# Five of eight output stores put into the load ring, and the last weights cut into other pieces

## The chip, the cores and the metric

The kernel runs on one core of a Trainium2 chip. The metric is device microseconds of one execution: the median of several runs. One execution is also profiled; its span is the time from the first to the last instruction on the core, and its own time is a little longer than the span.

## The reference

Eight experts, each a two-layer network over 256 rows of its own; all tensors are float32.

```python
n_experts, capacity, hidden, expert_hidden = 8, 256, 512, 2048

def reference(x, w1, w2, b1, b2):
    h = np.matmul(x, w1) + b1[:, np.newaxis, :]
    h = np.maximum(h, 0)
    return (np.matmul(h, w2) + b2[:, np.newaxis, :]).astype(np.float32)
```

x is 8 x 256 x 512, w1 is 8 x 512 x 2048 and w2 is 8 x 2048 x 512. The weights are 4 MB for each expert and product, 67 MB in all; the output is 0.5 MB for each expert.

## The kernel before

**Loads.** The weights, and x of experts 2 to 7, are cast from float32 to float16 on their way into SBUF. Such DMAs are issued by GpSimd (lines 65, 71, 82 and 90) and go through one queue, q0 in the profile, in the order of issue; here it is called the ring. A w1 or w2 takes 2 MB in SBUF as float16. x of experts 0 and 1 and b1 come through the SyncE and ScalarE queues and are cast by VectorE.

**Products.** `first_product(e)` makes 16 groups of 4 matmuls (128x128 weights, 256 columns); each group's sum goes through ScalarE (bias and relu, line 117) into `hT[e]`. In its middle `transposes(e + 1)` turns the x of the next expert. `second_product(e)` starts two sums, one for each half of the rows (tb 0 and 1), with b2 (line 151) and adds 16 rows of w2 blocks to each (line 163; "rows" of w2 are the 16 values of j, 512 columns each). `store` then copies tb 0 with VectorE (line 130) and tb 1 with ScalarE (line 131) into a tile of `out_pool`, which has two buffers, and SyncE issues one DMA of 512 KB (line 137).

**Order.** Stage s runs `first_product(s)` and, three stages late (LAG), `second_product(s - 3)`. A list `loads` holds x, w1 and w2 in the order in which they are wanted, and at each stage `issue_until` writes out loads up to w1 of expert s + 2 and w2 of expert s - 1. Each w1, and each w2 but the last, has three buffers, so that GpSimd's issue waits until TensorE has done with the buffer's old content. GpSimd works through its issues in order; what stands behind a waiting one waits too. SyncE's stores wait in the same way for the two copies.

**The last expert.** Its w2 comes in six pieces in tiles of their own: rows 0-4, 4-8, 8-12 and 12-14 over all 512 columns, then rows 14-16 as two halves of 256 columns. There are two blocks of 256 columns with two sums each. When the piece with row 15 of a block has been added, that block is copied and stored, tb 0 by SyncE (line 134) and tb 1 by ScalarE's own queue (line 135). So ScalarE copies, issues, copies and issues.

Of the kernel before, what the change touches and what calls it, by code (L numbers as in the profile page):

```python
# [11 lines left out]
def kernel(  # L12
# [9 lines left out]
    nc = tc.nc  # L22
    fp32 = mybir.dt.float32
    fp16 = mybir.dt.float16
    E, T, H = x.shape
    M = w1.shape[2]
    P = 128
    nTB = T // P
    nKC = H // P
    nJ = M // P  # L30
    HH = H // 2
    LAG = 3
    nXF32 = 2

    def ordered(ins):
        return tc.keep_in_program_order(ins)

    singles = ctx.enter_context(tc.tile_pool(name="singles", bufs=1))
    w1_pool = ctx.enter_context(tc.tile_pool(name="w1", bufs=3))
    w2_pool = ctx.enter_context(tc.tile_pool(name="w2", bufs=3))  # L40
    w2t_pool = ctx.enter_context(tc.tile_pool(name="w2t", bufs=1))
    x_pool = ctx.enter_context(tc.tile_pool(name="xp", bufs=4))
    xT_pool = ctx.enter_context(tc.tile_pool(name="xTp", bufs=2))
    hT_pool = ctx.enter_context(tc.tile_pool(name="hT", bufs=LAG + 2))
    out_pool = ctx.enter_context(tc.tile_pool(name="outp", bufs=2))
    psum_x = ctx.enter_context(tc.tile_pool(name="psum_x", bufs=1, space=bass.MemoryType.PSUM))
    psum_h = ctx.enter_context(tc.tile_pool(name="psum_h", bufs=3, space=bass.MemoryType.PSUM))
    psum_o = ctx.enter_context(tc.tile_pool(name="psum_o", bufs=2, space=bass.MemoryType.PSUM))
# [10 lines left out]
    w1_sb = [None] * E  # L59
    w2_sb = [None] * E  # L60
    hT = [None] * E

    def load_x(e):
        x16[e] = x_pool.tile([P, nTB, H], fp16, tag="x16", name="x16")
        ordered(nc.gpsimd.dma_start(  # L65
            out=x16[e], in_=x[e].rearrange("(p tb) h -> p tb h", tb=nTB)
        ))
# [7 lines left out]
    def load_w2(e):  # L75
        src = w2[e].rearrange("(p j) h -> p j h", j=nJ)
        w2_sb[e] = []
        if e < E - 1:
            t = w2_pool.tile([P, nJ, H], fp16, tag="w2", name="w2sb")
            step = nJ if e < E - 2 else nJ // 2  # L80
            for lo in range(0, nJ, step):
                ordered(nc.gpsimd.dma_start(out=t[:, lo : lo + step, :], in_=src[:, lo : lo + step, :]))  # L82
                w2_sb[e].append((lo, lo + step, 0, H, t[:, lo : lo + step, :]))
            return
        for lo, hi, c0, c1 in (
            (0, 4, 0, H), (4, 8, 0, H), (8, 12, 0, H), (12, 14, 0, H),
            (14, 16, 0, HH), (14, 16, HH, H),
        ):
            t = w2t_pool.tile([P, hi - lo, c1 - c0], fp16, tag=f"w2_{lo}_{c0}", name=f"w2_{lo}_{c0}")
            ordered(nc.gpsimd.dma_start(out=t, in_=src[:, lo:hi, c0:c1]))  # L90
            w2_sb[e].append((lo, hi, c0, c1, t))

    def transposes(e):
        pt = psum_x.tile([P, nKC, T], fp16, tag="psx", name="psx")
        for kc in range(nKC):
            for tb in range(nTB):
                ordered(nc.tensor.transpose(  # L97
                    out=pt[:, kc, tb * P : (tb + 1) * P],
                    in_=x16[e][:, tb, :].rearrange("p (q kc) -> p q kc", kc=nKC)[:, :, kc],
                    identity=ident16,  # L100
                ))
        xT[e] = xT_pool.tile([P, nKC, T], fp16, tag="xT", name="xT")
        nc.vector.tensor_copy(out=xT[e], in_=pt)  # L103

    def first_product(e):
        hT[e] = hT_pool.tile([P, nJ, T], fp16, tag="hT", name="hT")
        for j in range(nJ):
            ph = psum_h.tile([P, T], fp32, tag="ph", name="ph")
            for kc in range(nKC):
                ordered(nc.tensor.matmul(  # L110
                    out=ph,
                    lhsT=w1_sb[e][:, kc, :].rearrange("p (q j) -> p q j", j=nJ)[:, :, j],
                    rhs=xT[e][:, kc, :],
                    start=(kc == 0),
                    stop=(kc == nKC - 1),
                ))
            nc.scalar.activation(  # L117
                out=hT[e][:, j, :],
                in_=ph,
                func=mybir.ActivationFunctionType.Relu,  # L120
                bias=b1T[:, j, e : e + 1],
                scale=1.0,
            )
            if j == nJ // 2 and e + 1 < E:
                transposes(e + 1)

    def store(e, po, c0, c1, split):
        w = c1 - c0
        out_sb = out_pool.tile([P, nTB, w], fp32, tag=f"out{w}", name=f"out{w}")
        nc.vector.tensor_copy(out=out_sb[:, 0, :], in_=po[0])  # L130
        nc.scalar.copy(out=out_sb[:, 1, :], in_=po[1])  # L131
        dst = out[e].rearrange("(p tb) h -> p tb h", tb=nTB)[:, :, c0:c1]
        if split:
            nc.sync.dma_start(out=dst[:, 0, :], in_=out_sb[:, 0, :])
            nc.scalar.dma_start(out=dst[:, 1, :], in_=out_sb[:, 1, :])  # L135
        else:
            nc.sync.dma_start(out=dst, in_=out_sb)

    def second_product(e):
        if e < E - 1:  # L140
            blocks = [(0, H, psum_o, "po")]
        else:
            blocks = [(0, HH, psum_o, "po"), (HH, H, psum_h, "ph")]
        acc = {}
        for c0, c1, pool, tag in blocks:
            for tb in range(nTB):
                t = pool.tile(
                    [P, c1 - c0], fp32, tag=tag if tag == "ph" else f"{tag}{tb}", name=f"acc{tb}"
                )
                acc[c0, tb] = t  # L150
                ordered(nc.tensor.matmul(  # L151
                    out=t,
                    lhsT=ones1,
                    rhs=b2_sb[0:1, e * H + c0 : e * H + c1],
                    start=True,
                    stop=False,
                ))
        for lo, hi, p0, p1, t in w2_sb[e]:
            mine = [b for b in blocks if p0 <= b[0] and b[1] <= p1]
            for tb in range(nTB):  # L160
                for j in range(lo, hi):
                    for c0, c1, _, _ in mine:
                        ordered(nc.tensor.matmul(  # L163
                            out=acc[c0, tb],
                            lhsT=hT[e][:, j, tb * P : (tb + 1) * P],
                            rhs=t[:, j - lo, c0 - p0 : c1 - p0],
                            start=False,
                            stop=(j == nJ - 1),
                        ))
            if hi == nJ:  # L170
                for c0, c1, _, _ in mine:
                    store(e, [acc[c0, tb] for tb in range(nTB)], c0, c1, e == E - 1)

    x32 = singles.tile([P, nXF32, nTB, H], fp32)
    for e in range(nXF32):
# [4 lines left out]
        out=b2_sb,  # L180
        in_=b2.rearrange("e h -> (e h)").rearrange("(o f) -> o f", o=1),
# [10 lines left out]
    for j in range(nJ):  # L192
        for s in range(2):
            ordered(nc.tensor.matmul(  # L194
                out=pb[s * 64 : (s + 1) * 64, j, :, :],
# [5 lines left out]
    for s in range(2):  # L201
        nc.vector.tensor_copy(  # L202
            out=b1T[s * 64 : (s + 1) * 64, :, :], in_=pb[s * 64 : (s + 1) * 64, :, :, s]
        )
    transposes(0)

    loads = []
    for s in range(1, E + LAG):
        if s < E:
            if s >= nXF32:  # L210
                loads.append((load_x, s))
            loads.append((load_w1, s))
        if s >= LAG:
            loads.append((load_w2, s - LAG))
    n = 0

    def issue_until(done):
        nonlocal n
        while n < len(loads) and not done():
            loads[n][0](loads[n][1])  # L220
            n += 1

    for s in range(E + LAG):
        issue_until(lambda: (
            (min(s + 2, E - 1) < E and w1_sb[min(s + 2, E - 1)] is not None)
            and (s + 2 < LAG or w2_sb[min(s + 2 - LAG, E - 1)] is not None)
        ))
        if s < E:
            first_product(s)
        if s >= LAG:  # L230
            second_product(s - LAG)


# [28 lines left out]
```

## Time and profile before

| | |
|---|---|
| median of 3 runs | 186.31 us (185.98 to 186.66) |
| profiled execution: its time / its span | 185.88 us / 183.9 us |
| busy: TensorE / ScalarE / VectorE / GpSimd | 75% / 34% / 7% / 9% |
| DMA: moved, mean rate | 40.57 MB, 221 GB/s |
| HBM read / written | 71.39 MB / 4.19 MB |
| mean granted TensorE clock | 0.922 |

The profile's page gives for each engine a busy time, and cuts the span into 40 slices with a digit for each (9 is 90% busy or more). For DMA it gives the mean busy share of the core's 16 DMA engines and the bytes per second; a casting load counts with what it writes, half of what it reads. A second table gives packets, megabytes and share of the DMA engines for each queue: q0 is the GpSimd ring, q1 SyncE's queue and q10 ScalarE's. The chain of work that ended last goes back from the last instruction, at each step to what released it. In a timeline a line gives the start, the length, the engine, the line of the kernel, what is written from what, how many instructions are merged, and in brackets the idle time before and what ended it. The trace also holds one record for each DMA packet (queue, size written, start, length) and the moment at which each DMA's landing was signalled; where a text speaks of packet records or landings, it means these.

Some groups of the page (line, engine, operation, count, busy time, mean of one in ns, idle time before it and its releaser):

```profile
L110 PE MATMUL ph<-xT,w1sb 128*128 128x256 f16 x512 | 69.3, 302 | 11.8 <-DMA w1sb<-in_w_dram 11.8
L117 ACT ACTIVATE hT<-ph,b1T 128x256 f16<-128x256 f32 x128 | 57.1, 475 | 47.4 <-PE ph L110 47.1
L163 PE MATMUL acc<-w2sb,hT 128*128 128x512 f16 x224 | 49.7, 379 | 1.5 <-DMA w2sb<-in_w_dram 1.5
L90 POOL DMA_DIRECT2D w<-in_w_dram x6 | 3.6, 614 | 12.4 <-DMA w2sb<-in_w_dram 12.4
```

### The profile page before, as it was taken

To read this page: it belongs to the slowest core of one execution; us is meant where nothing else is said; L and a number is where in the kernel's file an instruction comes from. 1 tells how busy PE (TensorE), PEld (TensorE's weight loads), DVE (VectorE), ACT (ScalarE), POOL (GpSimd) and SP (SyncE) were. 2 spreads that over 40 slices of the span, in tenths; PEclk is the share of its full clock that TensorE was granted. 3 is DMA by queue.
4 is the path that set the end of the run, shared out by engine and by line. 5 is a ranking of instruction groups with operands and counts; after the bars stand their busy time and mean duration, and the time that the engine had idled before them with its cause. 6 is when DMAs were issued, how large, how long until landed. Compare 5 with 4: busy or idle time off the path is not lost.

```text
span 183.9 us, 2209 instructions
## 1 busy us (share of the span) xinstructions
PE 138.5 (75%) x946; PEld 99.0 (54%) x946; DVE 13.4 (7%) x22; ACT 62.8 (34%) x138; POOL 16.9 (9%) x37
## 2 busy tenths in 40 slices
PE   0546969397571999529995499917999997999971
PEld 0634969396451846427465464815648842434760
DVE  0320101001000100001010101001010010101001
ACT  0022869477360513605126150622506901010101
POOL 7100030301100012000110000100006200000000
PEclk9999999999875699965999789995799999999998
DMA  5998999899998999899999999999899998999993
GB/s 185 286 221 180 228 228 224 174 229 230 228 217 182 228 228 228 178 278 217 196 214 236 270 203 203 228 271 228 185 228 228 211 275 198 237 243 257 217 211 114
DMA packets 6488, 40.57 MB, mean 221 GB/s; under 512 B 688, under 2 KB 1728, under 8 KB 4432
## 3 DMA queue, kind: packets, MB, share of 16 engines
q0 software_dynamic: 4320, 35.14, 91.3%
q1 hardware_dynamic: 1568, 4.46, 6.6%
q10 hardware_dynamic: 592, 0.85, 1.3%
q8 instruction: 7, 0.11, 0.2%
q14 instruction: 1, 0.01, 0.0%
HBM read 71.39 MB, written 4.19 MB: 411 GB/s over the span
## 4 chain that ended last, share of the span: by engine, by line
DMA 57%; PE 31%; another core or an unknown queue 5%; POOL 3%; issue 1%; ACT 0%; ACTq 0%; POOLq 0%
DMA x<-in_x_dram 25%; DMA w<-in_w_dram 19%; PE ph L110 16%; DMA w1sb<-in_w_dram 12%; PE acc L163 12%; PE psx L97 2%; PE acc L151 1%; POOL w2sb L82 1%; POOL w L90 1%; POOL w1sb L71 1%; ACT out L131 0%; POOL b_sb L179 0%; POOL ident masks.py:199 0%; ACTq L135 0%
## 5 line engine op out<-in xcount | busy, mean ns | idle before, releaser
L110 PE MATMUL ph<-xT,w1sb 128*128 128x256 f16 x512 | 69.3, 302 | 11.8 <-DMA w1sb<-in_w_dram 11.8
L117 ACT ACTIVATE hT<-ph,b1T 128x256 f16<-128x256 f32 x128 | 57.1, 475 | 47.4 <-PE ph L110 47.1
L110 PEld LDWEIGHTS <-w1sb 128*128 128x128 f16 x512 | 62.0, 149 | 18.5 <-DMA w1sb<-in_w_dram 12.8
L163 PE MATMUL acc<-w2sb,hT 128*128 128x512 f16 x224 | 49.7, 379 | 1.5 <-DMA w2sb<-in_w_dram 1.5
L163 PEld LDWEIGHTS <-hT 128*128 128x128 f16 x288 | 27.5, 98 | 32.0 <-issue 6.5
L131 ACT COPY out<-acc 128x512 f32<-128x512 f32 (+1 forms) x9 | 4.9, 541 | 59.7 <-PE acc L163 59.7
L97 PE MATMUL psx<-ident,x 128*128 128x128 f16 x64 | 6.8, 269 | 20.6 <-DMA x<-in_x_dram 20.0
L97 PEld LDWEIGHTS <-x 128*128 128x128 f16 x64 | 5.3, 128 | 21.7 <-DMA x<-in_x_dram 20.9
L103 DVE COPY xT<-psx 128x1024 f16<-128x1024 f16 x8 | 5.5, 692 | 84.3 <-PE psx L97 84.3
L130 DVE COPY out<-acc 128x512 f32<-128x512 f32 (+1 forms) x9 | 5.7, 632 | 74.0 <-PE acc L163 73.9
L71 POOL DMA_DIRECT2D w1sb<-in_w_dram x8 | 4.4, 554 | 67.9 <-PE ph L110 67.1
L82 POOL DMA_DIRECT2D w2sb<-in_w_dram x8 | 4.3, 536 | 57.1 <-PE acc L163 57.1
L194 PE MATMUL pb<-ident,b_rows 16*64 16x16 f32 x64 | 3.7, 266 | 6.4 <-DMA b_rows<-in_b_dram 6.4
L163 PE MATMUL acc<-w,hT 128*128 128x256 f16 x64 | 7.6, 272 | 1.2 <-DMA w<-in_w_dram 1.2
L194 PEld LDWEIGHTS pb<-ident,b_rows 16*64 16x64 f32 x64 | 3.6, 198 | 6.4 <-issue 6.4
L117 ACT ACT_TABLE_LOAD x1 | 1.3, 1283 | 10.9 <-DVE b1T L202 10.9
L151 PE MATMUL acc<-b_sb,ones 1*128 1x512 f16 (+1 forms) x18 | 4.8, 355 | 0.0
L90 POOL DMA_DIRECT2D w<-in_w_dram x6 | 3.6, 614 | 12.4 <-DMA w2sb<-in_w_dram 12.4
L65 POOL DMA_DIRECT2D x<-in_x_dram x6 | 3.3, 546 | 2.2 <-DMA w1sb<-in_w_dram 2.2
L151 PEld LDWEIGHTS <-ones 1*128 1x128 f16 x18 | 1.1, 92 | 2.1 <-issue 2.1
L189 DVE CAST x<-x 128x1024 f16<-128x1024 f32 x2 | 1.4, 698 | 4.3 <-DMA x<-in_x_dram 4.3
L202 DVE COPY b1T<-pb 64x128 f32<-64x128 f32 x2 | 0.6, 288 | 3.5 <-PE pb L194 3.5
(8 smaller groups left out, 2.0 us busy)
## 6 DMA issues: line engine op xcount, KB each, us to landing
w1sb<-in_w_dram POOLq DMA_DIRECT2D x8, 2048.0 KB, 33.6
w2sb<-in_w_dram POOLq DMA_DIRECT2D x6, 2048.0 KB, 47.0
out_dram<-out SPq DMA_DIRECT2D x7, 512.0 KB, 8.0
w2sb<-in_w_dram POOLq DMA_DIRECT2D x2, 1024.0 KB, 24.3
x<-in_x_dram POOLq DMA_DIRECT2D x6, 256.0 KB, 39.9
w<-in_w_dram POOLq DMA_DIRECT2D x3, 512.0 KB, 31.8
x<-in_x_dram ACTq DMA_DIRECT2D x1, 512.0 KB, 5.2
x<-in_x_dram SPq DMA_DIRECT2D x1, 512.0 KB, 4.5
```

Of the source, the lines that this page charges most:

```text
L71: ordered(nc.gpsimd.dma_start(out=w1_sb[e], in_=w1[e].rearrange("(p kc) m -> p kc m", kc=nKC)))
L82: ordered(nc.gpsimd.dma_start(out=t[:, lo : lo + step, :], in_=src[:, lo : lo + step, :]))
L90: ordered(nc.gpsimd.dma_start(out=t, in_=src[:, lo:hi, c0:c1]))
L97: ordered(nc.tensor.transpose(out=pt[:, kc, tb * P : (tb + 1) * P], in_=x16[e][:, tb, :].rearrange("p (q kc) -> p q kc", kc=nKC)[:, :, kc] ...
L103: nc.vector.tensor_copy(out=xT[e], in_=pt)
L110: ordered(nc.tensor.matmul(out=ph, lhsT=w1_sb[e][:, kc, :].rearrange("p (q j) -> p q j", j=nJ)[:, :, j], rhs=xT[e][:, kc, :], start=(kc == 0),
L117: nc.scalar.activation(out=hT[e][:, j, :], in_=ph, func=mybir.ActivationFunctionType.Relu, bias=b1T[:, j, e : e + 1], scale=1.0,)
L130: nc.vector.tensor_copy(out=out_sb[:, 0, :], in_=po[0])
L131: nc.scalar.copy(out=out_sb[:, 1, :], in_=po[1])
L151: ordered(nc.tensor.matmul(out=t, lhsT=ones1, rhs=b2_sb[0:1, e * H + c0 : e * H + c1], start=True, stop=False,))
L163: ordered(nc.tensor.matmul(out=acc[c0, tb], lhsT=hT[e][:, j, tb * P : (tb + 1) * P], rhs=t[:, j - lo, c0 - p0 : c1 - p0], start=False, sto ...
L194: ordered(nc.tensor.matmul(out=pb[s * 64 : (s + 1) * 64, j, :, :], lhsT=b1_rows.rearrange("r (q j) -> r q j", j=nJ)[:, :, j], rhs=ident[0 ...
```

## The change

- **Stores.** With `RING = 4`, the stores of experts 0 to 4 are no longer issued by SyncE. `store` keeps destination and tile in `pending`, and `flush` issues them from GpSimd, at a fixed place of the ring: the store of expert e stands right behind the load of w2 of expert e + 3 (for e up to 3), and that of expert 4 behind the first piece of the last w2. The stores of experts 5 and 6 stay with SyncE (`PARTS` is empty, so in one DMA). `out_pool` has three buffers.
- **Pieces.** The last w2 comes in eight pieces: rows 0-4, 4-7, 7-10 and 10-12 over all columns, then rows 12-14 and 14-16 of columns 0 to 320 (`HL`), and rows 12-14 and 14-16 of columns 320 to 512.
- **Last stores.** The blocks are 320 and 192 columns wide. The block of 320 is stored by one SyncE DMA for both tb, and only the block of 192 is split between SyncE and ScalarE. Their tiles lie in `singles`.
- **Order.** The list is now `ring`, and each entry has the stage from which it may be written out; the first piece of the last w2 is written out one stage earlier.

```diff
-    HH = H // 2
+    HL = 320
     LAG = 3
+    RING = 4
+    PARTS = {}
...
-    out_pool = ctx.enter_context(tc.tile_pool(name="outp", bufs=2))
+    out_pool = ctx.enter_context(tc.tile_pool(name="outp", bufs=3))
...
+    def load_w2_piece(e, lo, hi, c0, c1):
+        t = w2t_pool.tile([P, hi - lo, c1 - c0], fp16, tag=f"w2_{lo}_{c0}", name=f"w2_{lo}_{c0}")
+        src = w2[e].rearrange("(p j) h -> p j h", j=nJ)
+        ordered(nc.gpsimd.dma_start(out=t, in_=src[:, lo:hi, c0:c1]))
+        if w2_sb[e] is None:
+            w2_sb[e] = []
+        w2_sb[e].append((lo, hi, c0, c1, t))
...
+    def flush(e):
+        dst, src = pending.pop(e)
+        ordered(nc.gpsimd.dma_start(out=dst, in_=src))
+
     def store(e, po, c0, c1, split):
         w = c1 - c0
-        out_sb = out_pool.tile([P, nTB, w], fp32, tag=f"out{w}", name=f"out{w}")
+        pool = out_pool if w == H else singles
+        out_sb = pool.tile([P, nTB, w], fp32, tag=f"out{c0}_{w}", name=f"out{w}")
         nc.vector.tensor_copy(out=out_sb[:, 0, :], in_=po[0])
         nc.scalar.copy(out=out_sb[:, 1, :], in_=po[1])
         dst = out[e].rearrange("(p tb) h -> p tb h", tb=nTB)[:, :, c0:c1]
-        if split:
+        if split and c1 == H:
             nc.sync.dma_start(out=dst[:, 0, :], in_=out_sb[:, 0, :])
             nc.scalar.dma_start(out=dst[:, 1, :], in_=out_sb[:, 1, :])
+        elif e <= RING:
+            pending[e] = (dst, out_sb)
         else:
-            nc.sync.dma_start(out=dst, in_=out_sb)
+            step = P // PARTS.get(e, 1)
+            for lo in range(0, P, step):
+                nc.sync.dma_start(out=dst[lo : lo + step], in_=out_sb[lo : lo + step])
...
-            blocks = [(0, HH, psum_o, "po"), (HH, H, psum_h, "ph")]
+            blocks = [(0, HL, psum_o, "po"), (HL, H, psum_h, "ph")]
...
+    ring = []
+    for s in range(1, E + LAG - 1):
         if s < E:
             if s >= nXF32:
-                loads.append((load_x, s))
-            loads.append((load_w1, s))
+                ring.append((s - 2, load_x, (s,)))
+            ring.append((s - 2, load_w1, (s,)))
         if s >= LAG:
-            loads.append((load_w2, s - LAG))
...
+            ring.append((s - 2, load_w2, (s - LAG,)))
+        if s >= 2 * LAG:
+            ring.append((s - 2, flush, (s - 2 * LAG,)))
+    e = E - LAG - 1
+    for piece in (
+        (0, 4, 0, H), (4, 7, 0, H), (7, 10, 0, H), (10, 12, 0, H),
+        (12, 14, 0, HL), (14, 16, 0, HL), (12, 14, HL, H), (14, 16, HL, H),
+    ):
+        ring.append((0, load_w2_piece, (E - 1,) + piece))
+        if e <= RING:
+            ring.append((e + LAG + 1, flush, (e,)))
+            e += 1
 
     for s in range(E + LAG):
...
+        while ring and ring[0][0] <= s:
+            _, put, args = ring.pop(0)
+            put(*args)
```

More of the change, by code (lines that the diff above doesn't have):

```diff
@@ L61 @@
     hT = [None] * E
+    pending = {}
     def load_x(e):
@@ L77, in load_w2 @@
         w2_sb[e] = []
[L78 to L91, printed above, removed]
+        t = w2_pool.tile([P, nJ, H], fp16, tag="w2", name="w2sb")
+        step = nJ if e < E - 2 else nJ // 2
+        for lo in range(0, nJ, step):
+            ordered(nc.gpsimd.dma_start(out=t[:, lo : lo + step, :], in_=src[:, lo : lo + step, :]))
+            w2_sb[e].append((lo, lo + step, 0, H, t[:, lo : lo + step, :]))
+    def load_w2_piece(e, lo, hi, c0, c1):
[5 more added lines that the diff above has]
+        w2_sb[e].append((lo, hi, c0, c1, t))
     def transposes(e):
@@ L205 @@
     transposes(0)
-    loads = []
-    for s in range(1, E + LAG):
+    ring = []
+    for s in range(1, E + LAG - 1):
         if s < E:
             if s >= nXF32:
-                loads.append((load_x, s))
-            loads.append((load_w1, s))
+                ring.append((s - 2, load_x, (s,)))
+            ring.append((s - 2, load_w1, (s,)))
         if s >= LAG:
-            loads.append((load_w2, s - LAG))
[L215 to L221, printed above, removed]
+            ring.append((s - 2, load_w2, (s - LAG,)))
[10 more added lines that the diff above has]
+            e += 1
     for s in range(E + LAG):
[L224 to L227, printed above, removed]
+        while ring and ring[0][0] <= s:
+            _, put, args = ring.pop(0)
+            put(*args)
         if s < E:
@@ L231 @@
             second_product(s - LAG)
+    assert not ring and not pending
 _INS = ['x', 'w1', 'w2', 'b1', 'b2']
```

## The prediction

> **What bounds the kernel now.** I read the page's slices and queue table first, then the chain that ended last, then the timelines of GpSimd's issues and of the last six microseconds, and last the trace's own records of DMA packets and landings. From the page, the DMA slices and the two queues that matter (packets, MB, share of 16 engines):
>
> ```profile
> DMA  5998999899998999899999999999899998999993
> ...
> q0 software_dynamic: 4320, 35.14, 91.3%
> q1 hardware_dynamic: 1568, 4.46, 6.6%
> ```
>
> The DMA engines are full from the second slice to the last but one. q0 is the GpSimd ring, which does the casting loads in order; q1 is SyncE, which does the stores. TensorE is busy 75%, so it isn't the bound. The chain agrees. Its end (start, length, what):
>
> ```profile
> 142.34 35.74 DMA w<-in_w_dram
> 178.08 0.04 issue
> 178.12 1.48 PE acc L163 x12
> 179.60 0.02 issue
> 179.63 0.38 ACT out L131
> 180.01 0.02 issue
> 180.03 0.37 ACTq L135
> 180.40 0.04 issue
> 180.44 0.37 ACT out L131
> ```
>
> So the span is: bytes through the DMA engines until the last w2 piece lands (179.43 by the landing records), then a tail of 183.9 - 179.43 = 4.5 us. Only two things can move the end: the engine time of what goes before that landing, and the tail. The landing records also show that time is additive: one 2 MB load follows the other by 9.68 us, and loads that a store runs beside are later by 1.33 us (w1, w2 of expert 4 and w2 of expert 5 together: landings 125.40 to 155.78 = 30.38, less 3 x 9.68). The last three stores add 3.95 us in all, 1.32 each.
>
> **The tail, in the timeline** (start, length, engine, line):
>
> ```profile
> 179.41 0.90 DVE L130 COPY out<-acc 128x256 f32<-128x256 f32 x2 [9.52 <-PE acc L163]
> 179.63 0.37 ACT L131 COPY out<-acc 128x256 f32<-128x256 f32 x1 [8.13 <-PE acc L163]
> 179.86 0.81 SPq L134 DMA_DIRECT2D out_dram<-out  x2
> 180.03 0.37 ACTq L135 DMA_DIRECT2D out_dram<-out  x1
> 180.44 0.37 ACT L131 COPY out<-acc 128x256 f32<-128x256 f32 x1 [0.44 <-PE acc L163]
> 180.84 0.35 ACTq L135 DMA_DIRECT2D out_dram<-out  x1
> ```
>
> TensorE ends at 180.07, but ScalarE starts its last copy at 180.44: it was issuing the first half's store until 180.40. Its last store is issued at 180.84 and lands at 182.90; 1.0 us later the span ends.
>
> **Part 1, stores 0 to 4 into the ring.** The same 2.5 MB go through the same 16 engines; none is moved behind the last load. So the gain is only what a store costs more beside the ring than in it. Beside it: 1.33 us (above; its 4 KB packets take 172 ns, eight per engine). In the ring no store is shown. Nearest row: the load of an x, which also moves 128 packets and reads 512 KB. It takes 1.23 to 1.26 us from landing to landing (57.71 to 58.97), because a packet in one ring starts about 17 ns before the one ahead of it is through (8 x 172 = 1.38 against 1.25). I take **1.25**. Lower bound 8 x (159 - 17) = 1.14, 159 ns being the store packet with nothing beside it. Upper bound 1.33 + 0.35 = 1.68, if the ring stands still from a store's completion packet to its landing (80.90 to 81.25 for store 0). Here the skill speaks against the change: "DMA: Bandwidth & Descriptors" (Anatomy of one DMA) puts most of a DMA's 2 us of fixed cost down to the write receipt, with HBM the heaviest target. A ring that waited for it would lose up to 5 x 2 = 10 us (an estimate from that page). The trace doesn't: a load into SBUF has 0.33 us there (25.84 to 26.17), a store into HBM 0.35, and 9.68 us is just 8 packets of 1.227 us less the overlap, so completions don't stop the ring. Sum: 5 x (1.25 - 1.33) = **-0.40** (-0.95 to +1.75).
>
> What the moves do elsewhere costs nothing while the ring is deep. GpSimd issues five stores and two pieces more, 7 x 0.55 = 3.9 us, hidden because it waits most of the span; SyncE loses 5 issues of 0.33. Each moved store waits behind the w2 load ahead of it on GpSimd, and for the DVE and ScalarE copies, 0.3 to 0.7 us after TensorE frees the w2 buffer. One wait is long: the store of expert 4 is behind the first piece, and its copies end near 151.5 (154.65 now, earlier since x of experts 5 to 7 no longer wait behind stores: 1.9, 3.3 and then 3.3 us). The other seven pieces stand behind it. They are now issued so:
>
> ```profile
> 139.75 1.06 POOL L82 DMA_DIRECT2D w2sb<-in_w_dram x2 [22.46 <-PE acc L163]
> 140.78 2.13 POOL L90 DMA_DIRECT2D w<-in_w_dram  x4
> 145.28 0.72 POOL L90 DMA_DIRECT2D w<-in_w_dram  x1 [2.36 <-DMA w2sb<-in_w_dram]
> 156.07 0.71 POOL L90 DMA_DIRECT2D w<-in_w_dram  x1 [10.07 <-DMA w2sb<-in_w_dram]
> ```
>
> The two waits show a second rule of this queue: the landing semaphores go round by eight, and an issue waits for the landing of the eighth before it (145.28 after w2 of expert 4 at 144.99; 156.07 after expert 5's at 155.78). Five stores more in the round move these partners. I walked it: x of expert 7 now waits for w2 of expert 1 (near 78), the store of expert 1 for w2 of expert 2 (near 99), the last piece for the first piece (near 169). At 151.5 the ring still holds w2 of expert 5, of 6, two stores and a piece: work until about 168. When the first piece lands, 8 us are queued. So no DMA engine goes empty, and the price is nil; with the cover gone it would be the whole wait. A third output buffer: expert 6's copy waits for the store of expert 3 to land, some 1.6 us after the second half of expert 6's w2, while its sum is ready 2.2 us after. Nil, and 1 us late would still let that store end ahead of the last piece.
>
> **Part 2, the pieces.** Packet records of the ring: 512 B takes 60 ns, 2048 B 172, 4096 B 324, 8192 B 624; that is 22 ns and 0.0735 ns per byte written, of which 17 ns overlap. Before: 3 x 8 x 307 ns, 8 x 155 and 2 x 16 x 43 = 7.37 + 1.24 + 1.38 = 9.99 us. After: 4 rows 2.46, twice 3 rows (3072 B, 231 ns) 3.70, 2 rows 1.24, two of 640 B 2 x 16 x 52 = 1.66, two of 384 B 2 x 16 x 33 = 1.06; sum 10.12. So **+0.13**. 384 B is below every data packet shown. The same page (Specifications) gives 512 B as the least for full rate, with a read-modify-write below. If that doubles them, +1.06 more (an estimate from that page). I take the line through the rows, as 512 B and even the 4 B completions (22 ns) lie on it; the page's price is the upper end.
>
> **Part 3, the tail.** TensorE's matmuls follow at 0.119 us for 256 columns (1.91 us for 16); 192 columns are held by the weight load, 98 ns. The last piece has 4, so the sums end 0.58 us after landing instead of 0.64. The 320 columns are summed before that (their last piece lands 1.06 us earlier; 4 x 0.145) and copied: by the two sizes shown, 256 and 512, ScalarE 0.43, DVE 0.49, all over 0.2 us after the last landing, and SyncE alone issues them. So ScalarE is free: copy of 192 columns 0.32, from 0.62 to 0.95, issue at 0.97 instead of 180.84 - 179.43 = 1.41. From issue to landing 2.06 stays, though 320 KB begin only 0.9 us ahead on the same engines; their 16 packets at about 55 ns end near 1.9. Landing at 3.0 instead of 3.47: **-0.47** (-0.65 if the smaller packets count in full, 0 if the large store holds the small ones back).
>
> **Sum:** -0.40 + 0.13 - 0.47 = -0.74. Span 183.9 to 183.2; the profiled execution 185.88 to 185.1; the median of the runs stands 0.43 above that execution, so 186.31 - 0.74 = **185.57**.
>
> **Rivals.** A change of 0.3% is 0.56 us, about what this kernel's measurements can tell.
> 1. In the ring a store costs the same 1.33: only pieces and tail count, -0.34, **185.97**. For it: transfer time dominates; against it: the overlap within one ring.
> 2. The 384 B packets are slow: -0.74 + 1.06 = +0.32, **186.63**. For it the page's rule, against it the line of the rows.
> 3. Slower: each moved store holds the ring until its completion is confirmed. Place: the five stores, each with loads behind it in the same ring; price 0.35 us each above 1.33, so +1.75 + 0.13 - 0.47 = +1.41, **187.7**. It decides from about 0.18 us per store on, where the sum passes +0.56. Against it: the equal 0.33 and 0.35 us, and loads that don't stop.
> 4. The ring runs dry behind the store of expert 4: needs 16 us of lateness, excluded by the walk but for an error in it.
>
> **How the numbers follow.** Likeliest 0.52 (own range 184.9 to 185.8, a tenth of it within 0.3%), rival 1 0.24 (a third of it faster, as the tail may give 0.65), rival 2 0.12 (half within, half slower with rival 1 beside it), rivals 3 and 4 together 0.12 (a tenth within). Faster 0.47 + 0.08 = 0.55; same 0.05 + 0.16 + 0.06 + 0.01 = 0.28; slower 0.06 + 0.11 = 0.17. Range 184.8 to 187.0: the lower end is the bound -0.95 + 0.13 - 0.65 = -1.47, the upper takes in rival 2 with rival 1 (+0.72) and leaves out most of rival 3.
>
> **What would show it.** Right: landing gaps of about 1.25 us for stores in q0; no gap in the DMA slices; a last ScalarE copy right behind TensorE's end with 192 columns; last landing near 179.1. Wrong: gaps after the ring's completion packets, 384 B packets well above 50 ns, GpSimd waiting with an empty ring, or the small last stores landing behind the 320 columns.

## The result, and the profile after

The changed kernel takes 185.63 us (median of 6 runs, 185.58 to 186.18) against 186.21 us before (6 runs); the ratio is 0.9973, 95% interval 0.9956 to 0.9990. Taken again beside other kernels on one chip it was 185.66 (12 runs) against 186.11 (29 runs), ratio 0.9977 (0.9963 to 0.9992). The forecast was 185.57, faster by 0.74 us. It is faster by 0.45 to 0.58 us: the direction is right and the size is 0.6 to 0.8 of the forecast. That the number came so near is luck in good part. The largest term of the sum, the tail, failed, a second came out right for another reason than the one given, and two that were not in the sum stand in their place.

The page after, the lines that answer to those shown of before (slices of DMA; queue: packets, MB, share):

```profile
DMA  5999999899999999999999999899999999999993
...
q0 software_dynamic: 5584, 37.76, 95.3%
q1 hardware_dynamic: 976, 2.00, 3.1%
```

The 2.5 MB went from q1 to q0, and the slices show the DMA engines as full as before, to the last but one. The ring never ran dry. GpSimd's issues near the end (timeline: start, length, what, idle time before and its releaser):

```profile
138.42 0.55 POOL L90 DMA_DIRECT2D w<-in_w_dram  x1
152.04 0.54 POOL L131 DMA_DIRECT2D out_dram<-out  x1 [13.07 <-ACT out L138]
152.57 0.54 POOL L90 DMA_DIRECT2D w<-in_w_dram  x1
153.43 0.53 POOL L90 DMA_DIRECT2D w<-in_w_dram  x1 [0.32 <-DMA w2sb<-in_w_dram]
154.68 0.53 POOL L90 DMA_DIRECT2D w<-in_w_dram  x1 [0.72 <-DMA out_dram<-out]
159.48 0.71 POOL L90 DMA_DIRECT2D w<-in_w_dram  x1 [4.27 <-DMA w2sb<-in_w_dram]
164.41 0.72 POOL L90 DMA_DIRECT2D w<-in_w_dram  x1 [4.22 <-DMA w2sb<-in_w_dram]
166.13 0.70 POOL L90 DMA_DIRECT2D w<-in_w_dram  x1 [1.00 <-DMA out_dram<-out]
169.34 0.71 POOL L90 DMA_DIRECT2D w<-in_w_dram  x1 [2.51 <-DMA w<-in_w_dram]
```

The long wait for the copies of expert 4 is there (13.07 us, until 152.04), and then all pieces but one wait for the landing of the eighth DMA before them. All of it is hidden, as the full slices show: the last piece is issued at 169.34 and lands at 179.31.

The end of the chain and the tail's timeline after:

```profile
153.43 21.99 DMA w<-in_w_dram
175.41 0.04 issue
175.45 3.88 PE acc L174 x32
179.34 0.02 issue
179.35 0.50 PE acc L174 x4
179.85 0.02 issue
179.88 0.32 ACT out L138
```

```profile
179.49 0.61 SPq L148 DMA_DIRECT2D out_dram<-out  x1
179.71 0.36 DVE L137 COPY out<-acc 128x192 f32<-128x192 f32 x1 [0.45 <-PE acc L174]
179.88 0.32 ACT L138 COPY out<-acc 128x192 f32<-128x192 f32 x1 [0.41 <-PE acc L174]
180.16 0.59 SPq L141 DMA_DIRECT2D out_dram<-out  x1
180.23 0.37 ACTq L142 DMA_DIRECT2D out_dram<-out  x1
```

The chain names an earlier piece, because TensorE was still at work when the last one landed at 179.31. But that landing counts: the last four matmuls start at 179.35, 0.26 us behind the one before them, where 0.08 is usual.

ScalarE's last copy does start right behind TensorE (179.88), and its store is issued at 180.23, 0.92 us after the last piece landed instead of 1.41. But the span ends at 183.8 all the same. The table of DMA issues says why (size, us from issue to landing):

```profile
out_dram<-out SPq DMA_DIRECT2D x1, 320.0 KB, 2.8
...
out_dram<-out SPq DMA_DIRECT2D x1, 96.0 KB, 2.7
out_dram<-out ACTq DMA_DIRECT2D x1, 96.0 KB, 2.4
```

Before, each of the last four stores landed 2.0 to 2.1 us after its issue. Now the small ones take 2.7 (SyncE's, from 180.16 to 182.88) and 2.4 (ScalarE's, from 180.23 to 182.59).

All profiled executions, cut at the same points (landing records; us). Each row is one execution, and the same kernel twice (after and e5) differs by up to 0.06:

| kernel | last w2 piece lands | from there to the last output landing | from there to the end of the span | outside the span |
|---|---|---|---|---|
| before | 179.43 | 3.47 | 1.03 | 1.95 |
| after | 179.31 | 3.57 | 0.93 | 1.77 |
| after, again (e5) | 179.25 | 3.58 | 0.91 | 1.78 |
| e1 ring only | 179.66 | 3.95 | 1.86 | 1.77 |
| e2 tail only | 179.90 | 3.76 | 1.10 | 2.13 |
| e3 scalar free | 179.64 | 3.81 | 1.10 | 1.94 |
| e4 320 from GpSimd | 179.26 | 3.79 | 2.35 | 1.77 |
| e6 two-part store | 179.39 | 3.57 | 1.35 | 1.8 |
| e7 block earlier | 179.30 | 2.86 | 0.92 | 1.8 |
| e8 all in ring | 179.17 | 3.57 | 0.92 | 1.8 |
| e9 both | 179.39 | 2.87 | 0.92 | 1.8 |
| e10 e1, one SyncE DMA less | 179.47 | 3.65 | 0.91 | 1.8 |
| e11 e1, piece in two | 179.22 | 3.51 | 1.77 | 1.8 |

For e6 to e11 the last column is the median over all of a kernel's runs, of a run's time less its span.

### The profile page after: what moved, and what is told of

Its sections match the earlier page's. It is cut to its first block, busy times and chain, and to the rows that moved or that the text cites. A ratio compares the mean times of both kernels' runs of the same rounds, so it can differ in the third digit from the quotient of the medians.

```text
span 183.8 us, 2205 instructions
## 1 busy us (share of the span) xinstructions
PE 137.3 (75%) x946; PEld 98.2 (53%) x946; DVE 13.3 (7%) x22; ACT 62.7 (34%) x138; POOL 21.0 (11%) x44
## 4 chain that ended last, share of the span: by engine, by line
DMA 70%; PE 14%; issue 9%; another core or an unknown queue 3%; POOL 2%; ACT 0%; POOLq 0%
DMA x<-in_x_dram 24%; DMA w2sb<-in_w_dram 21%; DMA w1sb<-in_w_dram 13%; DMA w<-in_w_dram 12%; PE ph L112 6%; PE acc L174 6%; PE psx L99 1%; POOL w2sb L84 1%; POOL w1sb L74 1%; POOL out_dram L131 0%; PE acc L162 0%; POOL b_sb L190 0%; POOL ident masks.py:199 0%; POOL ident masks.py:197 0%
## 5 line engine op out<-in xcount | busy, mean ns | idle before, releaser
L112 PE MATMUL ph<-xT,w1sb 128*128 128x256 f16 x512 | 68.2, 299 | 11.6 <-DMA w1sb<-in_w_dram 11.6
L138 ACT COPY out<-acc 128x512 f32<-128x512 f32 (+2 forms) x9 | 4.9, 543 | 62.0 <-PE acc L174 62.0
L137 DVE COPY out<-acc 128x512 f32<-128x512 f32 (+2 forms) x9 | 5.7, 632 | 75.5 <-PE acc L174 75.5
L174 PE MATMUL acc<-w,hT 128*128 128x320 f16 (+1 forms) x64 | 7.7, 272 | 3.8 <-DMA w<-in_w_dram 3.7
L90 POOL DMA_DIRECT2D w<-in_w_dram x8 | 5.0, 623 | 13.0 <-DMA w2sb<-in_w_dram 8.8
L131 POOL DMA_DIRECT2D out_dram<-out x5 | 2.7, 540 | 19.5 <-ACT out L138 13.1
L162 PE MATMUL acc<-b_sb,ones 1*128 1x512 f16 (+2 forms) x18 | 4.8, 355 | 0.0
```

The source lines that it names most:

```text
L112: ordered(nc.tensor.matmul(out=ph, lhsT=w1_sb[e][:, kc, :].rearrange("p (q j) -> p q j", j=nJ)[:, :, j], rhs=xT[e][:, kc, :], start=(kc == 0),
L162: ordered(nc.tensor.matmul(out=t, lhsT=ones1, rhs=b2_sb[0:1, e * H + c0 : e * H + c1], start=True, stop=False,))
L174: ordered(nc.tensor.matmul(out=acc[c0, tb], lhsT=hT[e][:, j, tb * P : (tb + 1) * P], rhs=t[:, j - lo, c0 - p0 : c1 - p0], start=False, sto ...
```

## The experiments

The kernels e1 to e4 ran on one chip, e5 to e8 on a second and e9 to e11 on a third, each group beside the kernel before; across groups, ratios to the kernel before are the ones to compare. "Theory A" and "Theory B" are those of the first two expectations: A says the gain is made in the ring, B that the tail makes it as the forecast's sum had it.

**e1_ring_only: the ring without the new pieces, blocks and last stores.**

```diff
-    HL = 320
+    HL = H // 2
...
-        if split and c1 == H:
+        if split:
...
-        (0, 4, 0, H), (4, 7, 0, H), (7, 10, 0, H), (10, 12, 0, H),
-        (12, 14, 0, HL), (14, 16, 0, HL), (12, 14, HL, H), (14, 16, HL, H),
+        (0, 4, 0, H), (4, 8, 0, H), (8, 12, 0, H), (12, 14, 0, H),
+        (14, 16, 0, HL), (14, 16, HL, H),
```

> Stores of experts 0 to 4 in the ring; pieces, blocks of 256 and last stores as before. Theory A (the gain is made in the ring, the tail gives nothing, since after the change it is still 4.5 us from the last landing to the end of the span): last w2 piece 0.3 to 0.4 us earlier than before relative to an early landing (the w1 of expert 4), tail 4.5 us, time 0.3 to 0.45 us under before, ratio 0.998. Theory B (the gain is the tail's, as the sum put it at 0.47, the ring gives nothing): last landing as before, time as before, ratio 1.000. Rival 3 of the prediction (completions hold the ring): slower by over 1 us.

Measured: 186.84 against 186.10, ratio 1.0037 (1.0024 to 1.0050). Neither theory. The profiled execution is the slowest of its six (187.24). The last piece lands no earlier than before (179.66 against 179.43), and both parts of the tail are longer, 3.95 and 1.86. In its timeline:

```profile
173.72 1.91 PE L174 MATMUL acc<-w,hT 128*128 128x256 f16 x16 [2.13 <-DMA w<-in_w_dram]
...
177.09 3.65 PE L174 MATMUL acc<-w,hT 128*128 128x256 f16 x32 [1.47 <-DMA w<-in_w_dram]
...
181.56 0.35 ACTq L142 DMA_DIRECT2D out_dram<-out  x1
```

The piece of rows 8 to 12 landed at 177.05 (175.73 before), as the store of expert 4 is now ahead of it in the ring and SyncE's store of expert 6 beside it. Behind it stood 32 matmuls, which TensorE did without a wait (the second line above), to 1.1 us after the last piece instead of 0.64. Here TensorE bounds the tail. The other part, 0.8 us between the last output landing and the end, is taken up at e6.

**e2_tail_only: new pieces, blocks and last stores; SyncE keeps all stores of experts 0 to 6.**

```diff
-    RING = 4
+    RING = -1
...
-        if s >= 2 * LAG:
+        if s >= 2 * LAG and s - 2 * LAG <= RING:
```

> Eight pieces, blocks of 320 and 192 and one SyncE store for the block of 320; all stores of experts 0 to 6 by SyncE as before. Theory A: last landing 0.1 us later to 0.1 earlier, tail 4.5 us, time as before within 0.15 us, ratio 1.000. Theory B: tail 4.0 us, time 0.35 to 0.5 under before, ratio 0.9975.

Measured: 186.73 against 186.10, ratio 1.0032 (1.0019 to 1.0045), slower by 0.63 us. Theory B falls, and A's "as before" too: the tail is longer, not shorter. In its timeline:

```profile
179.53 0.49 DVE L137 COPY out<-acc 128x320 f32<-128x320 f32 x1 [8.07 <-PE acc L174]
179.81 0.42 ACT L138 COPY out<-acc 128x320 f32<-128x320 f32 x1 [6.73 <-PE acc L174]
180.26 0.62 SPq L148 DMA_DIRECT2D out_dram<-out  x1
```

SyncE's store of expert 6 lands at 178.87 here, among the last pieces; in the changed kernel at 175.58. The second piece of the 320 columns lands 0.88 us ahead of the last piece instead of 1.05, and the large store is issued 0.36 us after the last landing instead of 0.18. So the new pieces alone lose and the ring alone (e1) loses; together they gain. What the executions show for it: in the changed kernel w2 of expert 6 lands 3 us earlier (164.13 against 167.14 here), and with it the store of expert 6 leaves the stretch in which the last pieces come.

**e3_scalar_free: before, with one SyncE DMA for the first block.**

```diff
-        if split:
+        if split and c1 == H:
```

> Before, with one change: the first block of 256 columns is stored by one SyncE DMA for both halves of the rows, so that ScalarE issues nothing between its last two copies. If ScalarE's issue alone set the tail, its last store is issued 0.35 to 0.4 us earlier and the tail falls from 4.5 to 4.1, ratio 0.998. If SyncE's queue takes its place (the large store's issue and its packets stand ahead of SyncE's small store), ScalarE's issue is as early but SyncE's last landing comes as late as ScalarE's did: tail 4.4 to 4.6, ratio 1.000.

Measured: 186.62 against 186.10, ratio 1.0030 (1.0019 to 1.0041). The timeline has what the forecast counted on, and what it missed:

```profile
180.04 0.61 SPq L137 DMA_DIRECT2D out_dram<-out  x1
...
180.32 0.37 ACT L131 COPY out<-acc 128x256 f32<-128x256 f32 x1 [0.30 <-PE acc L163]
180.72 0.39 ACTq L135 DMA_DIRECT2D out_dram<-out  x1
180.75 0.54 SPq L134 DMA_DIRECT2D out_dram<-out  x1
```

ScalarE's last store is issued 1.08 us after the last piece's landing instead of 1.41, as worked out. But SyncE takes 0.61 us to issue the large store instead of 0.33, and its small one behind it lands last, at 3.81 instead of 3.47. SyncE's queue took ScalarE's place and did worse.

**e4_320_from_gpsimd: the large store out of SyncE's queue.**

```diff
+        elif split:
+            ordered(nc.gpsimd.dma_start(out=dst, in_=out_sb))
         elif e <= RING:
```

> After, with the store of 320 columns issued by GpSimd, so that SyncE's and ScalarE's queues hold only their small stores. If SyncE's queue holds the small store back (its first packet comes 1.7 us after its issue, behind the last of the large store), SyncE's small store is issued 0.1 us earlier at about 0.8 us after the last piece's landing and its packets begin 0.3 us sooner; last landing of all 0.2 to 0.3 us earlier than after, tail 4.2 to 4.3, ratio to before 0.996. If the DMA engines themselves are the limit in the tail (all 512 KB of it), or GpSimd's issue is as late, the tail stays 4.5 and the ratio 0.997.

Measured: 187.21 against 186.10, ratio 1.0063 (1.0049 to 1.0078). In its timeline:

```profile
180.05 0.33 SPq L141 DMA_DIRECT2D out_dram<-out  x1
180.12 0.68 POOL L144 DMA_DIRECT2D out_dram<-out  x1 [10.54 <-DVE out L137]
180.17 0.37 ACTq L142 DMA_DIRECT2D out_dram<-out  x1
```

The small stores do land earlier now, both by 182.31 instead of 182.88, and they take 2.09 (SyncE's) and 2.14 us (ScalarE's) from issue to landing instead of 2.7 and 2.4: so the large store had held them back. But GpSimd issues the large one only at 180.12 (SyncE: 179.49), and it lands last, at 183.04. GpSimd then comes out of its last wait 1.1 us after SyncE has done with the landings (184.65 against 183.53). Here a GpSimd store as the last DMA costs more than it frees. Why GpSimd issued so late, after the copies were ready at 179.36, isn't settled.

**e5_after_again: the changed kernel beside the next three.**

> The changed kernel itself, beside the variants below on one chip. Ratio to before 0.997; span near 183.8 us, and 1.75 to 1.8 us outside the span, against 1.9 to 2.0 for before.

Measured: 185.66, ratio 0.9977 (0.9963 to 0.9992). As expected; its medians are used below: span 183.9 against 184.2, outside it 1.78 against 1.95.

**e6_two_part_store: one DMA more, far from the end.**

```diff
-    PARTS = {}
+    PARTS = {5: 2}
```

> The changed kernel with one edit: SyncE's store of expert 5 in two DMAs of 64 partitions (PARTS = {5: 2}), 170 us into the span and with the same bytes. Theory C: at the end SyncE tests eight landing semaphores in a fixed order, 0.06 us for each that stands behind the last to land; DMAs of SyncE's and ScalarE's queues take them in turn, so one DMA more moves the last small store from the last place of that order to the first. Then the end comes 7 x 0.062 = 0.43 us later than for the changed kernel, and all of it lies between the last landing and the end. Otherwise nothing changes: under 0.1 us.

Measured: 186.24 against 185.66 of e5, +0.58 us; ratio to before 1.0008 (0.9996 to 1.0020). In the profiled executions, 1.35 us lie between the last output landing and the end instead of 0.91. That is Theory C's 0.43 us, in its place; the 0.14 us more of the medians is not placed. The records of SyncE's last instructions (start in us, semaphore waited for):

```
182.97  landing semaphore 107   <- the last store to land, at 182.96
183.04  109
183.10  110
183.16  114
183.22  115
183.28  116
183.34  117
183.40  118
```

In the changed kernel the same store waits on semaphore 118, the last of the row. Before, the last store to land waited on 116, with two tests behind it. So splitting a store whose issue and landing were both hidden (it landed by 169.39, 15 us before the end) took back the whole gain of the change. The same order explains 0.31 us of e1 (nine such DMAs, so the first place) and 0.06 of e2 and e3 (fifth place). About 0.5 us more of e1's stretch, and 0.4 of e11's, lie in GpSimd's own last instructions: two that follow each other after 0.08 us elsewhere are 0.45 us apart in both. Why stays open.

**e7_block_earlier: the pieces of the 320 columns first.**

```diff
-        (0, 4, 0, H), (4, 7, 0, H), (7, 10, 0, H), (10, 12, 0, H),
-        (12, 14, 0, HL), (14, 16, 0, HL), (12, 14, HL, H), (14, 16, HL, H),
+        (0, 4, 0, H), (4, 8, 0, H), (8, 12, 0, HL), (12, 14, 0, HL),
+        (14, 16, 0, HL), (8, 12, HL, H), (12, 14, HL, H), (14, 16, HL, H),
```

> The changed kernel with other pieces: rows 0-4 and 4-8 whole, then rows 8-12, 12-14, 14-16 of the 320 columns, then the same rows of the 192 columns, so that the block of 320 is complete some 2.1 us before the last landing instead of 1.05. If the large store holds SyncE's small one back, its packets are now through about 1 us sooner: last output landing 2.7 to 3.0 us after the last piece's instead of 3.57, ratio to before 0.993. If the tail is set by issue and landing latency alone (2.1 us from the small store's issue), the tail falls by 0.2 at most; if the large store's packets now delay the last pieces by as much as they gain, the time is that of the changed kernel.

Measured: 185.21, ratio 0.9954 (0.9938 to 0.9971), 0.45 us under the changed kernel. The last output lands 2.86 us after the last piece instead of 3.57, and the last piece at the same time as in the changed kernel (179.30). Windows of the end, first of the changed kernel and then of e7 (the stretch and its length; busy time and count of TensorE, its weight loads, VectorE, ScalarE and GpSimd; granted clock, DMA share, GB/s):

```profile
178.00:179.50 1.50, 1.48 (x13) 0.98 (x12) 0.49 (x1) 0.43 (x1) 0.00 (x0) 1.00 0.36 42
179.50:181.00 1.50, 0.34 (x4) 0.11 (x2) 0.36 (x1) 0.32 (x1) 0.00 (x0) 1.00 0.15 53
181.00:182.50 1.50, 0.00 (x0) 0.00 (x0) 0.00 (x0) 0.00 (x0) 0.00 (x0) 1.00 0.92 302
```

```profile
178.00:179.50 1.50, 1.22 (x14) 1.16 (x14) 0.21 (x1) 0.42 (x1) 0.00 (x0) 1.00 0.33 38
179.50:181.00 1.50, 0.33 (x4) 0.10 (x2) 0.36 (x1) 0.32 (x1) 0.00 (x0) 1.00 0.64 228
181.00:182.50 1.50, 0.00 (x0) 0.00 (x0) 0.00 (x0) 0.00 (x0) 0.00 (x0) 0.97 0.40 127
```

In the changed kernel the DMA engines are nearly idle from 179.5 to 181.0 and full after that, when the small stores want to go. In e7 the large store fills that gap, and the small ones find the engines free. The small stores are issued hardly earlier after the last piece than in the changed kernel (0.79 and 0.92 us, against 0.85 and 0.92), but take 1.8 and 1.9 us to land. Together with e4 this shows the cause: the large store in front of them. How much of it is SyncE's own queue and how much the shared DMA engines is not separated; ScalarE's small store, in a queue of its own, was late too.

The executions differ by 0.71 us there and the medians by 0.45. The profiled execution of e7 is its fastest, and its pieces cost 0.24 us more by the packet times of the forecast (an estimate); which of the two counts is not shown.

**e8_all_stores_in_ring.**

```diff
-    RING = 4
+    RING = 6
```

> The changed kernel with RING = 6: the stores of experts 5 and 6 in the ring too, behind the second and third piece. Theory A (a store costs about 0.03 to 0.1 us less in the ring than beside it, and no longer delays the pieces beside it): last landing 0 to 0.2 us earlier; 0.12 us later at the end by theory C (sixth place of eight); outside the span 0.05 less: time as that of the changed kernel within 0.2 us. If GpSimd waiting for the copies of expert 6 near 168.5 us lets the ring run dry (it should still hold over 5 us of work), the last landing is later by 1 us or more and the DMA slices show a gap.

Measured: 185.62, ratio 0.9976 (0.9964 to 0.9988): as the changed kernel. No gap in the ring. The 0.12 us of the sixth place did not come (0.92 us to the end): with six such DMAs SyncE has only six tests, so the last store is again at the end of the row.

**e9_earlier_and_all: e7 and e8 together.**

```diff
-    RING = 4
+    RING = 6
```

(on top of e7's pieces)

> The pieces of e7_block_earlier together with RING = 6 of e8_all_stores_in_ring. If the two are independent: tail 3.7 to 3.8 us as in e7, last landing 0 to 0.2 us earlier than in e7, ratio to before 0.9945 (about 185.1 us). If the stores of experts 5 and 6 in the ring only delay the pieces that the block of 320 needs, the time is e7's or up to 0.2 us more.

Measured: 185.13 against 186.16, ratio 0.9955 (0.9941 to 0.9969). Tail as in e7 (2.87 and 0.92 us); the two stores more in the ring bring nothing that can be measured. e7 and e9 are both faster than before, and by about 0.5 us faster than the change.

**e10_ring_lane_moved: e1 with one SyncE DMA less.**

```diff
-    RING = 4
+    RING = 5
```

(on top of e1)

> e1_ring_only (pieces, blocks and last stores of before) with RING = 5, so one SyncE DMA less: the last ScalarE store moves from the first place of SyncE's eight final tests to the last. By theory C the time falls by 0.43 us against e1, to 186.3 to 186.4, and the stretch from the last output landing to the end is below 1.1 us. If e1 was slower for another reason alone (its matmuls ending 1.1 us after the last piece instead of 0.64), it stays at 186.8.

Measured: 186.37 (185.57 to 187.59, 12 runs), ratio 1.0020 (0.9997 to 1.0043). The median is 0.47 under e1's, but the runs scatter over 2 us, in two groups, and the intervals of the two ratios overlap, so the time by itself shows nothing. In the profiled execution the end comes 0.91 us after the last output landing instead of 1.86, which fits e6. What splits the runs is not known.

**e11_ring_piece_split: e1 with rows 8 to 12 in two pieces.**

```diff
-        (0, 4, 0, H), (4, 8, 0, H), (8, 12, 0, H), (12, 14, 0, H),
+        (0, 4, 0, H), (4, 8, 0, H), (8, 10, 0, H), (10, 12, 0, H), (12, 14, 0, H),
```

(on top of e1)

> e1_ring_only with its third piece (rows 8-12) in two, rows 8-10 and 10-12. In e1 this piece landed at 177.05, beside SyncE's store of expert 6, and TensorE then had 32 matmuls, 3.65 us without a wait, while the last piece landed at 179.66: TensorE ended 1.1 us after it. With the split, 24 matmuls or fewer stand behind the landing near 177, so TensorE ends about 0.65 us after the last piece: time 0.3 to 0.5 us under e1, 186.3 to 186.5. If the order of the final tests alone made e1 slow, it stays at 186.8.

Measured: 186.45 against 186.16, ratio 1.0019 (1.0008 to 1.0030), 0.39 us under e1 in the median, with intervals that overlap a little. In its timeline:

```profile
176.70 1.03 PE L174 MATMUL acc<-w,hT 128*128 128x256 f16 x8 [1.08 <-DMA w<-in_w_dram]
177.94 1.92 PE L174 MATMUL acc<-w,hT 128*128 128x256 f16 x16 [0.20 <-DMA w<-in_w_dram]
```

TensorE now waits for the last pieces again and ends 0.64 us after the last one instead of 1.1, and the last output lands 3.51 us after it instead of 3.95. So the 32 matmuls behind the late piece were a cause of e1's time, apart from the order of the final tests (1.77 us to the end here, still the first place).

## Why the prediction was right or wrong

**What bounds the kernel: right.** The DMA engines stay full, and the time is the last landing plus the tail.

**Part 1, stores in the ring.** The term was far too large; what is left of it lies within the scatter. Landing to landing, four of the moved stores take 1.32, 1.30, 1.26 and 1.31 us in the ring, mean 1.30, where the row of x had given 1.25 (expert 3's lies beside SyncE's store and can't be read). Against 1.33 that is -0.15 for five, not -0.40. Still the sum of parts 1 and 2 is about right, by luck. Counted from the landing of w1 of expert 4, the last piece lands after 110.78 to 111.07 us where SyncE has the stores (before, e2, e3; mean 110.95) and after 110.47 to 110.78 with the five in the ring and the new pieces (after, e4 to e7; mean 110.63): -0.32 against -0.27 foreseen. With -0.15 and +0.13 (part 2) only -0.02 of it is accounted for; e1, with the same five in the ring, took 111.02. The rest lies in a stretch not in the sum. From one to three microseconds before the first store's packets on, 16 to 29 of the 16 KB load packets of every execution take longer than 1.3 us, up to 1.6 to 2.3, instead of 1.23. This stretch cost 0.6 to 0.9 us in the three kernels with SyncE's stores and 0.2 to 0.65 in those five, but 1.1 in e1 and e10. So its difference is scatter as much as gain; its cause is open. Behind it, from the landing of w1 of expert 7 to the last piece, what the loads leave over is 1.32 to 1.34 us for each store where SyncE has them and 1.27 to 1.33 in after and e4 to e7 (an estimate from the load times of the forecast). Rival 1 (in the ring a store costs the same) was therefore nearer on the price than the forecast.

**Rivals 3 and 4: out.** x of expert 7 lands 1.23 us behind the store of expert 0 in the ring, just as long as behind a load: completions of stores don't hold the ring. The write receipt to which the Trainium skill ("DMA: Bandwidth & Descriptors", Anatomy of one DMA) puts down most of the fixed cost is latency here, and not time of the ring. The walk of GpSimd's waits was right nearly to the microsecond (151.5 foreseen and 152.04 found for the store of expert 4, 169 and 169.34 for the last piece).

**Part 2, the pieces: right.** 3072 B packets take 248 ns, 640 B 69 and 384 B 51 (line: 50). The last four pieces land 0.86, 0.80, 0.53 and 0.52 us apart, 2.71 in all, 2.72 worked out. No price below 512 B shows in these loads into SBUF (the doubling in rival 2 was the forecast's own assumption), so rival 2 is out.

**Part 3, the tail: wrong.** The step that failed is "From issue to landing 2.06 stays", and with it "Landing at 3.0 instead of 3.47: -0.47". The step before it held: ScalarE was free, and its issue came at 0.92 us (0.97 foreseen). But from issue to landing ScalarE's small store took 2.36 us and SyncE's 2.72. What the sum had no term for is the cost of the large store in the queue it was moved to. SyncE needs 0.61 us to issue the store of 256 rows of 1280 B (0.33 for a store of one tb); its first packet comes 1.26 us after the issue (0.83 before), its last ends at 181.82 instead of about 181.2, and SyncE's small store goes behind it (181.92). The landing was at 3.57, +0.10. The forecast had named this as the bound "0 if the large store holds the small ones back" and gave it too little weight. e3 shows it alone, and e4 and e7 take it away. A small term was off without effect: the matmuls of 192 columns follow each other at 0.083 us, not at the 0.098 of a weight load.

**What was not in the sum.** The step "1.0 us later the span ends" took that stretch for a constant. It depends on how many DMAs SyncE and ScalarE have issued in all: the change takes away five SyncE stores and two last ones become one, so the last store moved from the sixth place of SyncE's final tests to the eighth: -0.10 between the profiled executions (1.03 to 0.93), two tests of 0.062 us each as e6 has them. And outside the span the time fell from 1.95 to 1.78 us in the medians, -0.17. Kernels with ten SyncE DMAs have 1.93 to 2.05 there, those with three to six 1.75 to 1.81. Why is not shown.

The sum after the fact: -0.32 to the last landing, +0.10 to the last output landing, -0.10 to the end, -0.17 outside = -0.49, beside -0.45 and -0.58 measured. The forecast had -0.27, -0.47, 0 and 0. Of the measured sum, the -0.10 is shown by experiment; most of the -0.32 and the -0.17 have been measured but not explained.

In the forecast's working, the loads that land between 125.40 and 155.78 are w1 of expert 7 and w2 of experts 4 and 5; the sum drawn from them stands.

## What to carry to other kernels

Where the DMA engines are full to the end, look at the stretch after the last load as a schedule of its own: which large store's packets lie ahead of the small last ones, and whether the engines idle before that. Moving an issue off a busy engine pays only if the queue that takes it has room; cost its issue and its packets, not just the engine that is freed. A change that is meant for one place can gain or lose as much by the order in which the last landings are tested (0.44 us here), so compare the end of the span, behind the last landing, before a gain of half a microsecond is put down to anything else.

## What the runs showed of the hardware

- SyncE tests the landing semaphores of SyncE's and ScalarE's DMAs one after another at the end, 0.062 us each. One more hidden DMA put the last store from the end of the row to its start: +0.44 us between the last landing and the end, +0.58 us in the median.
- SyncE's issue of a store took 0.33 to 0.37 us for 128 rows of 0.75 to 4 KB and 0.59 to 0.62 us for 256 rows of 1 to 1.3 KB, and a small store issued right behind the large one took 0.54 to 0.59. The number of rows is not all of it: the two stores of 64 rows in e6 took 0.54 and 0.58.
- Just before the first store of an execution, wherever its packets come (76 or 118 us), 16 KB load packets stretched from 1.23 us to as much as 1.6 to 2.3, which delayed the ring by 0.2 to 1.1 us. The cause is open.
- A GpSimd store as the last DMA ended the span 2.35 us after its landing, against 0.9 to 1.9 where a SyncE or ScalarE store came last.
